# Output projection and second feed-forward of a transformer layer with token tiles as the stationary operand

## The chip, the cores and the metric

The kernel runs on one core of a Trainium2 chip. The metric is the device time of one execution in microseconds (us). A core has five engines with instruction queues of their own: PE (TensorE, matmuls, with weight loads shown as PEld), DVE (VectorE), ACT (ScalarE), POOL (GpSimd) and SP, which here starts DMAs. Matmuls write to PSUM, eight banks of 128 x 512 floats; everything else is kept in SBUF.

## The reference, cut to what matters

One layer on 256 latent tokens (and 256 context tokens, which end after the keys and values), width 2048, in float32:

```
x   = half_ffn(x, mod, 0, ...)                       # first ff, also for ctx
h   = modulate(rms_norm(x, g1), shift, scale)
q, k, v, hy = split(h @ w_in)
attn = attention(q, k, v)                            # 256 x 1024
hyo  = hyena(hy)                                     # 256 x 1024
y    = concat([rms_norm(attn, g_out[:1024]), rms_norm(hyo, g_out[1024:])])
x   = x + gate5 * (y @ w_out)                        # 2048 x 2048
h   = modulate(rms_norm(x, g2), shift6, scale7)
x   = x + 0.5 * gate8 * ((silu(h @ w_gate) * (h @ w_up)) @ w_down)   # 2048 -> 2 x 5632 -> 2048
```

The gates, shifts and scales are vectors over the 2048 features, computed from the conditioning inputs. A group's rms_norm divides each token by the root mean square over that group's 1024 features and multiplies each feature by its gain.

## The kernel before

All matrix products run in fp32r, each float split in a high part and a low rest; a product is hi*hi + hi*lo + lo*hi. Weights come from HBM in pieces of 512 KB (128 x 1024 floats, tile `raw`, four buffers, issued by SP). ACT casts the high part (`whi`, L192) and DVE, or for every second piece of the second ff's down POOL, subtracts it for the rest (`wlo`, L194); both have three buffers.

The residual `xs` is feature-major: 16 feature tiles of 128 partitions (`xd(0, d)`, L106) with the tokens along the free axis. A matmul holds a 128 x 128 piece of weights in the array and streams tokens. The first ff has latent and context tokens, 512 columns, three matmuls a piece (`mm3`, L201 to L203). From the Hyena projection on there are 256 tokens, and `mm2` (L205) streams the high and low parts of the tokens side by side past `whi` (512 columns, L209) and the high part alone past `wlo` (256 columns, L208 or L211): a pair per piece. The key/value and query projections (`proj_steps`, L644) already hold tokens in the array and stream 512 weight columns (L653 to L655).

The stages, in order: first ff; keys and values; Hyena projection (eight column tiles `ct`, L751); long convolution by DFT, with the queries in its gaps; attention, with the x0 gate of the Hyena branch filled in (`gate`, `fill`, FILL); the group norms (`group_out`, L877: squares on ACT, sums by a matmul against `ones` at L245, root and reciprocal on 128 x 256, scaling at L883, split at L181/L182); the output projection (`out_part`, L901, eight pairs of output tiles, the first three begun on the attention half alone); the norm of x (`col_rstd`), the modulation (L251 to L254) and the second ff. That one (`most`, L347) runs 44 up steps `j` of 64 pairs and after every fourth a down group of 64 pairs, whose 16 results are each multiplied by the gate and added to `xs` on DVE (L330, two per tile). Finished feature tiles are stored at the end.

Instructions are issued by Python in program order, but a scheduler of the tile framework then sets the order on each engine; engines run in that order and wait on semaphores. Tiles with tag `u` share 58 buffers of 2 KB per partition, PSUM has four `pa` and four `pb` banks.

Of the kernel before, what the change touches and what calls it, by code (L numbers as in the profile page):

```python
# [18 lines left out]
P = 128  # L19
D = 2048  # L20
# [6 lines left out]
OUT = (KT // 2, P, 2, L)  # L27
# [10 lines left out]
FILL = (1, 0, 3)  # L38
# [9 lines left out]
def hybrid_layer_kernel(ctx: ExitStack, tc: tile.TileContext, a):  # L48
# [220 lines left out]
    class Ffn:  # L269
        def __init__(self, nparts, wup, wdown, cm, hook=None):  # L270
            self.np, self.N, self.wup, self.wdown, self.cm = nparts, nparts * L, wup, wdown, cm
            self.hook = hook or (lambda: None)
            self.h = [None] * KT
            self.acts = {}
            self.gated = nparts == 1
            self.mm = mm2 if nparts == 1 else mm3
# [16 lines left out]
        def close(self, j, ps2):  # L293
            sg = tmp2((P, 2, L))
            if self.np == 2:
                S.activation(sg, ps2[0], AF.Silu)
                V.tensor_mul(sg, ps2[1], sg)
                self.acts[j] = split(sg, (P, 2, L))
                return
            for half in range(2):  # L300
                S.copy(sg[:, half, :], ps2[half][:, 1, :])
                V.tensor_add(sg[:, half, :], ps2[half][:, 0, :], sg[:, half, :])
            S.activation(sg[:, 0, :], sg[:, 0, :], AF.Silu)
            V.tensor_mul(sg[:, 1, :], sg[:, 0, :], sg[:, 1, :])
            self.acts[j] = U((P, 2, L), F32R)
            split_to(sg[:, 1, :], self.acts[j][:, 0, :], self.acts[j][:, 1, :])
# [7 lines left out]
        def down(self, g, parts=None, last=None):  # L314

            whole = parts is None
            for dq in range(KT // 2):
                self.hook()
                whi, wlo = weight(self.wdown[g, dq], (P, GRP, 2, P), G if dq % 2 and self.np == 1 else None)
                for i2 in range(2):  # L320
                    d = dq * 2 + i2
                    ps = PB((P, 2, L) if whole else (P, L))
                    for jj in range(GRP):
                        act = self.acts[g * GRP + jj]
                        if not whole:
                            act = [t[:, parts, :] for t in act]
                        self.mm(ps, (whi[:, jj, i2, :], wlo[:, jj, i2, :]), act, jj == 0, jj == GRP - 1)
                    if self.np == 1:
                        for half in range(2):
                            V.scalar_tensor_tensor(xd(0, d), ps[:, half, :], mod[0][8][:, d : d + 1], xd(0, d),  # L330
                                                   op0=ALU.mult, op1=ALU.add)
                        if last:
                            last(d)
                        continue
# [12 lines left out]
        def most(self, first):  # L347

            for j in range(first, JT):
                self.up(j)  # L350
                if j % GRP == 0 and j > 0:
                    self.down(j // GRP - 1)
# [132 lines left out]
    f1 = Ffn(2, a["w_up1"], a["w_dn1"], 0)  # L485
# [108 lines left out]
    mp = ctx.enter_context(tc.tile_pool(name="mp", bufs=1))  # L594
# [62 lines left out]
    def small(shape):  # L657
        return T(mp, shape, "small", bufs=8)

# [91 lines left out]
    for ct in range(CT):  # L751
# [5 lines left out]
        V.tensor_mul(vT[ct // 2][:, ct % 2, :], yv, y1)  # L757

# [118 lines left out]
    def group_out(src, g0, out):  # L877
        r_ = U((P, L))
        yield from rstd_steps(src, HW, r_)
        for i in range(4):  # L880
            t = T(up, (P, 2, L), "sq", bufs=2)
            for j in range(2):
                V.scalar_tensor_tensor(t[:, j, :], src[i][:, j, :], gout[:, g0 + 2 * i + j : g0 + 2 * i + j + 1], r_,  # L883
                                       op0=ALU.mult, op1=ALU.mult)
            for j in range(2):
                hl = U((P, 2, L), F32R)
                split_to(t[:, j, :], hl[:, 0, :], hl[:, 1, :])
                out.append(hl)
        yield

    y = []
    attn_out = group_out(attnT, 0, y)
    next(attn_out)
    fill(FILL[2])
    next(attn_out)
    for _ in gate:
        pass
    gate_out = group_out(hyT, CT, y)
    next(gate_out)

    def out_part(ps, dq, kqs):  # L901
        for kq in kqs:
            whi, wlo = weight(a["w_o"][dq, kq], (P, 4, 2, P))
            for i2 in range(2):
                for k4 in range(4):
                    k = kq * 4 + k4
                    mm2(ps[i2], (whi[:, k4, i2, :], wlo[:, k4, i2, :]), y[k], k == 0, k == KT - 1)

    def out_add(ps, dq):
        for i2 in range(2):  # L910
            d = dq * 2 + i2
            for half in range(2):
                V.scalar_tensor_tensor(xd(0, d), ps[i2][:, half, :], mod[0][5][:, d : d + 1], xd(0, d),
                                       op0=ALU.mult, op1=ALU.add)

    early = 3
    pso = [[f((P, 2, L)), f((P, 2, L))] for f in (PA, PA, PB)]
    for dq in range(early):
        out_part(pso[dq], dq, (0, 1))
        if dq == 0:  # L920
            next(gate_out)
    for dq in range(early):
        out_part(pso[dq], dq, (2, 3))
        out_add(pso[dq], dq)
    for dq in range(early, KT // 2):
        ps = [PA((P, 2, L)), PA((P, 2, L))]
        out_part(ps, dq, (0, 1, 2, 3))
        out_add(ps, dq)


    rs2 = U((P, L))
    col_rstd(xs[0], D, rs2)
    f2 = Ffn(1, a["w_up2"], a["w_dn2"], 6)
    f2.h = normed(0, rs2, 6)
    f2.most(0)

    def store(d):
        if d >= KT - 2:
            nc.sync.dma_start(a["out"][d // 2, :, d % 2, :], xd(0, d))
        elif d % 2:  # L940
            nc.sync.dma_start(a["out"][d // 2], xs[0][d // 2])

    f2.down(JT // GRP - 1, None, store)


# [37 lines left out]
def _prepare(i):  # L983
# [31 lines left out]
    for n in (1, 2):  # L1015
        d[f"w_up{n}"] = pair(i[f"w_ffn{n}_up"][0], JT)
        d[f"w_dn{n}"] = down(i[f"w_ffn{n}_down"][0])
# [5 lines left out]
    d["w_o"] = wide(i["w_out"][0])  # L1023
# [32 lines left out]
```

## Time and profile before

| | |
|---|---|
| median of three runs | 2728.03 us (2726.80 to 2729.72) |
| the profiled execution | 2727.58 us |
| its span | 2725.7 us |
| TensorE clock granted, mean | 0.993 |
| HBM read | 506.98 MB, 188 GB/s over the span |
| first ff until about | 1545 us |
| key/value projections to the end of attention | 1545 to 1843 us |
| group norms and output projection | 1843 to 1959 us |
| second ff | 1968 to 2722 us |

A row of the timeline gives the start and the duration of an instruction (or of several merged, x4), its engine, line and operation, what it writes and reads by name (numbers of buffers left out), and in brackets how long the engine was idle before it and who ended that. Matmuls are pipelined, so their durations overlap, and the distance of starts is what one costs. A row of the groups gives count, busy time, mean nanoseconds of one, and idle time before them. A row of the windows gives the stretch, its length, busy time and count of PE, the granted clock and the DMA share.

### The profile page before, as it was taken

What the parts mean: (1) busy time and instruction counts of PE and PEld (TensorE: products, weight loads), DVE (VectorE), ACT (ScalarE), POOL (GpSimd) and SP (SyncE); (2) the same over time, 40 slices, a digit from 0 to 9 for tenths busy, and PEclk for the clock granted to TensorE, in tenths of its full rate; (3) what the DMA queues carried; (4) which work ended last, traced back from release to release, by engine and by line L of the source; (5) the groups of instructions that cost most, each with busy time, mean ns of one, the idle gap of its engine ahead of it and who ended that gap; (6) DMA issues with size and microseconds to landing.
All of it is one profiled execution on the core that took longest, in us unless ns stands there. A gap on an engine that the chain in (4) does not pass through costs nothing.

```text
span 2725.7 us, 35248 instructions
## 1 busy us (share of the span) xinstructions
PE 2677.7 (98%) x13552; PEld 2231.1 (82%) x13552; DVE 1870.3 (69%) x3106; ACT 963.0 (35%) x1307; POOL 108.7 (4%) x51
## 2 busy tenths in 40 slices
PE   8999999999999999999999999998999999999999
PEld 5678888888888888888888878887788888888888
DVE  6589898976696666433343886988666666666666
ACT  4343222222222222222222555465454444444443
POOL 0000000000000000000000000000011111111111
PEclk9999999999999999999999999999999999999999
DMA  9776666665686666432323455333455555555555
GB/s 383 284 267 211 225 215 218 214 231 202 228 290 236 212 220 215 160 100 93 101 93 101 134 176 186 116 116 132 155 179 187 185 185 185 186 186 185 185 185 170
DMA packets 144352, 513.49 MB, mean 188 GB/s; under 512 B 17175, under 2 KB 21432, under 8 KB 139832
## 3 DMA queue, kind: packets, MB, share of 16 engines
q1 hardware_dynamic: 142456, 508.50, 54.8%
q10 hardware_dynamic: 1728, 2.74, 0.3%
q8 instruction: 107, 1.75, 0.3%
q14 instruction: 61, 0.50, 0.1%
HBM read 506.98 MB, written 4.19 MB: 188 GB/s over the span
## 4 chain that ended last, share of the span: by engine, by line
PE 94%; DVE 5%; DMA 1%; ACT 1%; issue 0%; ACTq 0%; SPq 0%; DVEq 0%
PE pa L209 17%; PE pa L203 11%; PE pa L201 11%; PE pa L202 11%; PE pa L211 8%; PE pb L201 7%; PE pb L203 7%; PE pb L202 6%; PE pb L209 6%; PE pb L211 2%; DVE u L182 1%; PE pa L654 1%; PE pa L655 1%; PE pb L157 1%; PE pa L653 1%; PE pb L208 1%
## 5 line engine op out<-in xcount | busy, mean ns | idle before, releaser
L192 ACT CAST whi<-raw 128x1024 fp32r<-128x1024 f32 x648 | 680.8, 1051 | 1310.2 <-PE pa L202 469.9
L194 DVE TENSOR_TENSOR wlo<-raw,whi 128x1024 fp32r<-128x1024 f32 x601 | 734.5, 1223 | 507.4 <-ACT whi L192 495.7
L209 PE MATMUL pa<-u,whi 128*128 128x512 f32 x2016 | 713.6, 400 | 12.7 <-DVE u L254 5.9
L201 PE MATMUL pa<-u,whi 128*128 128x512 f32 x1376 | 537.8, 392 | 0.9 <-ACT u L529 0.9
L202 PE MATMUL pa<-u,whi 128*128 128x512 f32 x1376 | 536.8, 390 | 0.7 <-DVE u L531 0.7
L203 PE MATMUL pa<-u,wlo 128*128 128x512 f32 x1376 | 535.6, 390 | 1.5 <-DVE wlo L194 1.5
L211 PE MATMUL pa<-u,wlo 128*128 128x256 f32 x1890 | 532.4, 282 | 0.8 <-DVE wlo L194 0.8
L209 PEld LDWEIGHTS pa<-u,whi 128*128 128x128 f32 x2016 | 377.2, 189 | 100.6 <-issue 6.3
L211 PEld LDWEIGHTS pa<-u,wlo 128*128 128x128 f32 x1890 | 358.9, 190 | 4.8 <-DVE wlo L194 1.7
L201 PEld LDWEIGHTS pa<-u,whi 128*128 128x128 f32 x1376 | 258.6, 188 | 58.4 <-issue 3.5
L203 PEld LDWEIGHTS pa<-u,wlo 128*128 128x128 f32 x1376 | 258.3, 188 | 57.0 <-DVE wlo L194 2.4
L202 PEld LDWEIGHTS pa<-u,whi 128*128 128x128 f32 x1376 | 259.0, 188 | 55.3 <-DVE u L531 1.6
L201 PE MATMUL pb<-u,whi 128*128 128x512 f32 (+1 forms) x800 | 298.7, 374 | 0.3 <-ACT u L176 0.3
L203 PE MATMUL pb<-u,wlo 128*128 128x512 f32 (+1 forms) x800 | 296.9, 372 | 1.0 <-DVE wlo L194 1.0
L202 PE MATMUL pb<-u,whi 128*128 128x512 f32 (+1 forms) x800 | 297.5, 372 | 0.0
L209 PE MATMUL pb<-u,whi 128*128 128x512 f32 x736 | 250.4, 399 | 2.2 <-DVE u L330 2.2
L130 DVE CUSTOM_DVE_ANT_0 adas<-adaw,crow,bada 128x1024 bf16<-128x1024 f32 x160 | 205.1, 1282 | 17.9 <-DMA adaw<-in_w_adaT_dram 15.8
L130 DVE CUSTOM_DVE_ANT_0 adas<-adaw,crow,mod 128x1024 bf16<-128x1024 f32 x160 | 205.2, 1283 | 10.4 <-DMA adaw<-in_w_adaT_dram 7.4
L194 POOL TENSOR_TENSOR wlo<-raw,whi 128x1024 fp32r<-128x1024 f32 x44 | 107.7, 2448 | 2607.7 <-ACT whi L192 2607.7
L201 PEld LDWEIGHTS pb<-u,whi 128*128 128x128 f32 x800 | 150.8, 189 | 31.5 <-issue 4.8
L203 PEld LDWEIGHTS pb<-u,wlo 128*128 128x128 f32 x800 | 150.4, 188 | 27.5 <-DVE wlo L194 1.2
L202 PEld LDWEIGHTS pb<-u,whi 128*128 128x128 f32 x800 | 150.9, 189 | 26.1
(202 smaller groups left out, 2249.6 us busy)
## 6 DMA issues: line engine op xcount, KB each, us to landing
raw<-in_w_up_dram SPq DMA_DIRECT2D x352, 512.0 KB, 3.6
adaw<-in_w_adaT_dram SPq DMA_DIRECT2D x223, 512.0 KB, 4.9
raw<-in_w_dn_dram SPq DMA_DIRECT2D x184, 512.0 KB, 3.5
wrow<-in_w_ada_dram SPq DMA_DIRECT2D x32, 1024.0 KB, 7.9
raw<-in_w_hy_dram SPq DMA_DIRECT2D x32, 512.0 KB, 3.5
raw<-in_w_o_dram SPq DMA_DIRECT2D x32, 512.0 KB, 3.5
raw<-in_w_kv_dram SPq DMA_DIRECT2D x16, 512.0 KB, 3.5
raw<-in_w_q_dram SPq DMA_DIRECT2D x16, 512.0 KB, 3.5
```

Of the source, the lines that this page charges most:

```text
L130: V.tensor_tensor_reduce(out=sc, in0=t, in1=crow[i][:, b * (D // 2) : (b + 1) * (D // 2)], scale=1.0, scalar=mcol if b else bada[:, n : n ...
L157: PE.matmul(bank[g : g + 32, 0 : 2 * P], cs[:, k, :], t[:, k8, :], start=k < 4, stop=k >= KT - 4)
L182: V.tensor_sub(lo, src, hi.bitcast(F32))
L192: S.copy(hi, raw)
L194: (eng or V).tensor_sub(lo, raw, hi.bitcast(F32))
L201: PE.matmul(ps, w[0], xx[0], start=start, stop=False)
L202: PE.matmul(ps, w[0], xx[1], start=False, stop=False)
L203: return PE.matmul(ps, w[1], xx[0], start=False, stop=stop)
L208: PE.matmul(ps[:, 0, :], w[1], x[:, 0, :], start=start, stop=False)
L209: PE.matmul(ps, w[0], x, start=start, stop=stop)
L211: PE.matmul(ps[:, 0, :], w[1], x[:, 0, :], start=False, stop=False)
L653: PE.matmul(p_, hh, whi[:, k2, :], start=k == 0, stop=False)
```

## The change

The output projection and the second ff take the form of `proj_steps`: `tok_mm` holds 128 tokens of one feature tile in the array and streams 512 weight columns, three matmuls for each of two token halves. Their results are token-major (128 tokens x 512 features), and so is the residual from there on: during the Hyena projection PE transposes it, one group of four 128 x 128 tiles per `ct`, into `xt`. The gates 5 and 8 are transposed too, written to HBM and loaded as rows broadcast over all partitions (`gate_row`).

The group norms move to the read-out: `group_in` only multiplies by the gain and splits; `group_rstd` sums the squares per token with two-column matmuls, and `out_add` multiplies the finished 128 x 512 block by the token's factor and the gate row and adds it to `xt`. The projection is eight units: four column blocks for the attention half, then four for the Hyena half. The norm of x comes from squares with a row sum (128 x 2 values per factor), and the normed x is transposed back for the array. Sixteen small matmuls (`AWAKE2`) follow the last of the projection.

The second ff runs 22 up units of 512 columns (256 of the gate half, 256 of the up half), transposes each unit's product during the next unit, and keeps all activations in SBUF; then down runs in four column blocks over all 44 activation tiles, each summed in PSUM to its end, multiplied by the gate row, added to `xt` and stored. POOL splits no weights any more.

```diff
-FILL = (1, 0, 3)
+FILL = (1, 0)
+AWAKE2 = 16
+EXTRA = 14
...
+    def turn_x(t, b):
+        ps = PB((P, 4, P))
+        for i in range(4):
+            PE.transpose(ps[:, i, :], xd(0, 4 * b + i)[:, t * P : (t + 1) * P], ident)
+        xt[t][b] = U((P, 512))
+        S.copy(xt[t][b], ps.rearrange("p a b -> p (a b)"))
...
+        turn_x(ct % 2, ct // 2)
+        if ct == 4:
+            turn_gates()
...
-    def group_out(src, g0, out):
-        r_ = U((P, L))
-        yield from rstd_steps(src, HW, r_)
...
+    def group_in(src, g0):
...
+                S.activation(hl[:, 0, :], src[i][:, j, :], AF.Copy, scale=gout[:, k : k + 1])
+                V.scalar_tensor_tensor(hl[:, 1, :], src[i][:, j, :], gout[:, k : k + 1], hl[:, 0, :].bitcast(F32),
+                                       op0=ALU.mult, op1=ALU.subtract)
+            sq = (tmp2 if i == 0 else tmp)((P, 2, L))
+            S.activation(sq, src[i], AF.Square)
...
+    def group_rstd(acc):
+        ps = PB((P, 2, 2))
+        for t in range(2):
             for j in range(2):
+                PE.matmul(ps[:, t, :], acc[:, j, t * P : (t + 1) * P], ones[:, 0:2], start=j == 0, stop=j == 1)
...
+    def tok_mm(ps, x, w, start, stop):
+
+        for t in range(2):
+            hi, lo = (x_[:, t * P : (t + 1) * P] for x_ in x)
+            PE.matmul(ps[t], hi, w[0], start=start, stop=False)
+            PE.matmul(ps[t], hi, w[1], start=False, stop=False)
+            last = PE.matmul(ps[t], lo, w[0], start=False, stop=stop)
+        return last
...
+    def out_add(ps, r_, b):
+        for t in range(2):
+            o = tmp2((P, 512))
+            V.scalar_tensor_tensor(o, ps[t], r_[:, t : t + 1], grow[b], op0=ALU.mult, op1=ALU.mult)
+            V.tensor_add(xt[t][b], xt[t][b], o)
...
+    for b in range(NB):
+        ps, last = out_unit(1, b)
+        out_add(ps, rh, b)
+        for t in range(2):
+            S.activation(tmp((P, 512)), xt[t][b], AF.Square, accum_out=sumsq[:, t, b : b + 1])
...
+    spin = PA()
+    with tc.issue_after(last.ins):
+        for _ in range(AWAKE2):
+            last = PE.matmul(spin[:, 0:P], ones, ones, start=True, stop=True)
...
+            for i in range(2):
+                d = 4 * b + 2 * i2 + i
+                sc, sh = mod[0][7][:, d : d + 1], mod[0][6][:, d : d + 1]
+                hl, m_ = U((P, 2, L), F32R), T(up, (P, L), "mt", bufs=3)
+                S.activation(hl[:, 0, :], pt[:, i, :], AF.Identity, bias=sh, scale=sc)
+                V.tensor_scalar(m_, pt[:, i, :], sc, sh, op0=ALU.mult, op1=ALU.add)
+                V.tensor_sub(hl[:, 1, :], m_, hl[:, 0, :].bitcast(F32))
...
+            if kp == 2 and prev:
+                turn_act(*prev)
+        at = U((P, 2, L))
+        for t in range(2):
+            sg = tmp2((P, L))
+            S.activation(sg, ps[t][:, 0:L], AF.Silu)
+            V.tensor_mul(at[:, t, :], ps[t][:, L : 2 * L], sg)
...
+        for t in range(2):
+            o = tmp2((P, 512))
+            V.tensor_mul(o, ps[t], grow[b])
+            V.tensor_add(xt[t][b], xt[t][b], o)
+            nc.sync.dma_start(a["out"][t, :, b * 512 : (b + 1) * 512], xt[t][b])
```

Three places of the new order. First PE within up of the second ff, before: `pa` are the PSUM tiles of one up step, `u` an input feature tile, `whi` and `wlo` the weights.

```order
L209 MATMUL pa_2967_15592<-u_2935_15512,whi_2970_15596 128x512
L211 MATMUL pa_2967_15592<-u_2935_15512,wlo_2971_15597 128x256
L209 MATMUL pa_2968_15593<-u_2935_15512,whi_2970_15596 128x512
L211 MATMUL pa_2968_15593<-u_2935_15512,wlo_2971_15597 128x256
L209 MATMUL pa_2967_15592<-u_2937_15517,whi_2970_15596 128x512
```

And now, in the second up unit, at the sixth of its sixteen k-tiles; `pb_3055` takes the transposes of the unit before (`u_3041`):

```order
L924 MATMUL pa_3045_15748<-whi_3053_15787,u_2984_15506 128x512
L925 MATMUL pa_3045_15748<-wlo_3054_15788,u_2984_15506 128x512
L926 MATMUL pa_3045_15748<-whi_3053_15787,u_2984_15506 128x512
L1011 MATMUL pb_3055_15803<-ident_1_67,u_3041_15740 128x128 x4
L924 MATMUL pa_3044_15747<-whi_3059_15814,u_2987_15516 128x512
L925 MATMUL pa_3044_15747<-wlo_3060_15815,u_2987_15516 128x512
```

Pairs of 512 and 256 columns have become triples of 512, and four transposes stand once per unit in PE's queue.

Second DVE where the output projection begins, before: `L182` are low parts of the scaled group, `L194` weight splits, `L913` the first adds to the residual.

```order
L182 TENSOR_TENSOR u_2821_14767<-sq_2820_14764,u_2821_14767 128x256
L194 TENSOR_TENSOR wlo_2837_14864<-raw_2835_14861,whi_2836_14863 128x1024
L182 TENSOR_TENSOR u_2822_14770<-sq_2820_14764,u_2822_14770 128x256
L194 TENSOR_TENSOR wlo_2840_14886<-raw_2838_14883,whi_2839_14885 128x1024
L194 TENSOR_TENSOR wlo_2843_14912<-raw_2841_14909,whi_2842_14911 128x1024
L194 TENSOR_TENSOR wlo_2846_14934<-raw_2844_14931,whi_2845_14933 128x1024
L913 SCALAR_TENSOR_TENSOR u_32_117<-pa_2797_14675,mod0_5_19_102,u_32_117 128x256 x2
```

Now, with `L901` and `L908` of the Hyena group's `group_in`, `L941` and `L942` the read-out of the projection's first unit, and `wlo_2842` the first split of its second unit:

```order
L901 SCALAR_TENSOR_TENSOR u_2833_14821<-u_2419_13089,gout_1761_9352,u_2833_14821 128x256
L901 SCALAR_TENSOR_TENSOR u_2834_14824<-u_2419_13089,gout_1761_9352,u_2834_14824 128x256
L908 TENSOR_TENSOR sg_2826_14801<-sg_2826_14801,sq_2835_14827 128x512
L941 SCALAR_TENSOR_TENSOR sg_2836_14830<-pa_2810_14721,small_2807_14712,u_2802_14699 128x512
L941 SCALAR_TENSOR_TENSOR sg_2837_14833<-pa_2811_14722,small_2807_14712,u_2802_14699 128x512
L942 TENSOR_TENSOR u_2273_12294<-u_2273_12294,sg_2836_14830 128x512
L942 TENSOR_TENSOR u_2293_12406<-u_2293_12406,sg_2837_14833 128x512
L200 TENSOR_TENSOR wlo_2842_14841<-raw_2840_14838,whi_2841_14840 128x1024
```

The splits of the next unit stood ahead of the first adds; now its first split stands behind the group's work and the whole read-out.

Third PE at the joint from the projection to the second ff, before: `pb_2924` is the sum of squares of x.

```order
L211 MATMUL pa_2910_15382<-u_2821_14767,wlo_2922_15452 128x256
L208 MATMUL pa_2910_15382<-u_2822_14770,wlo_2922_15452 128x256
L209 MATMUL pa_2910_15382<-u_2822_14770,whi_2921_15451 128x512
L245 MATMUL pb_2924_15476<-sg_2925_15477,ones_2_72 128x256 x2
L245 MATMUL pb_2924_15476<-sq_2932_15497,ones_2_72 128x256 x2
L209 MATMUL pa_2967_15592<-u_2935_15512,whi_2970_15596 128x512
```

Now, with the spin at `L969` and `u_2967`, `u_2968` the normed x of the two token halves:

```order
L926 MATMUL pa_2945_15343<-whi_2956_15400,u_2834_14824 128x512
L969 MATMUL pa_2962_15430<-ones_2_72 128x128 x16
L991 MATMUL pb_2969_15462<-ident_1_67,u_2967_15458 128x128
L991 MATMUL pb_2974_15477<-ident_1_67,u_2967_15458 128x128
L991 MATMUL pb_2969_15462<-ident_1_67,u_2968_15460 128x128
L991 MATMUL pb_2969_15462<-ident_1_67,u_2967_15458 128x128
L991 MATMUL pb_2969_15462<-ident_1_67,u_2968_15460 128x128
L991 MATMUL pb_2974_15477<-ident_1_67,u_2968_15460 128x128
L991 MATMUL pb_2974_15477<-ident_1_67,u_2967_15458 128x128
L991 MATMUL pb_2974_15477<-ident_1_67,u_2968_15460 128x128
L924 MATMUL pa_3015_15594<-whi_3018_15598,u_2970_15467 128x512
```

The two sums over all features are gone from PE; sixteen small matmuls and eight transposes of the normed x stand between the projection and the first up matmul.

More of the change, by code (lines that the diff above doesn't have):

```diff
@@ L294, in close @@
             sg = tmp2((P, 2, L))
[L295 to L306, printed above, removed]
+            S.activation(sg, ps2[0], AF.Silu)
+            V.tensor_mul(sg, ps2[1], sg)
+            self.acts[j] = split(sg, (P, 2, L))
         def up(self, j):
@@ L318, in down @@
                 self.hook()
-                whi, wlo = weight(self.wdown[g, dq], (P, GRP, 2, P), G if dq % 2 and self.np == 1 else None)
+                whi, wlo = weight(self.wdown[g, dq], (P, GRP, 2, P))
                 for i2 in range(2):
@@ L658, in small, with turn_gates, gate_row @@
         return T(mp, shape, "small", bufs=8)
+    xt = [[None] * NB for _ in range(2)]
+    def turn_x(t, b):
[4 more added lines that the diff above has]
+        S.copy(xt[t][b], ps.rearrange("p a b -> p (a b)"))
+    gate_rows = T(dram, (2, KT, P), "gate_rows")
+    def turn_gates():
+        ps, rows = PB((KT, 2, P)), tmp((KT, 2, P))
+        for n, c in enumerate((5, 8)):
+            PE.transpose(ps[:, n, :], mod[0][c], ident)
+        S.copy(rows, ps)
+        nc.scalar.dma_start(gate_rows.rearrange("n k p -> k n p"), rows)
+    def gate_row(n):
+        out = []
+        for b in range(NB):
+            out.append(U((P, 512)))
+            nc.sync.dma_start(out[b], gate_rows[n : n + 1, 4 * b : 4 * b + 4, :].rearrange("n k p -> n (k p)").partition_broadcast(P))
+        return out
     def head_norm(ps, nh):
@@ new lines, in tok_mm, with out_unit @@
+    def tok_mm(ps, x, w, start, stop):
[5 more added lines that the diff above has]
+        return last
+    def out_unit(g, b):
+        ps = [PA(), PA()]
+        for kp in range(4):
+            whi, wlo = weight(a["w_o"][b, 4 * g + kp], (P, 2, 512))
+            for k2 in range(2):
+                k = 2 * kp + k2
+                last = tok_mm(ps, [y[8 * g + k][:, s, :] for s in range(2)], (whi[:, k2, :], wlo[:, k2, :]), k == 0, k == 7)
+        return ps, last
@@ L896, in hybrid_layer_kernel @@
+    def out_add(ps, r_, b):
[3 more added lines that the diff above has]
+            V.tensor_add(xt[t][b], xt[t][b], o)
+    acc = group_in(attnT, 0)
     for _ in gate:
         pass
[L898 to L907, printed above, removed]
@@ L925, in hybrid_layer_kernel @@
[L925 to L943, printed above, removed]
+    grow = gate_row(0)
@@ L1022, in _prepare @@
     d["w_x0"] = wide(c_(wi[:, 1536:2560]))
-    d["w_o"] = wide(i["w_out"][0])
+    d["w_o"] = np.stack([cols(c_(i["w_out"][0][:, b * 512 : (b + 1) * 512])) for b in range(NB)])
     def eo(v):
```

140 lines of the change are left out of this document (91 added, 49 removed).

## The prediction

> **What bounds the kernel now.** I read the page first (busy time, then the chain that ended last), then windows for whole stages, then the timeline for the distance from one matmul's start to the next.
>
> ```profile
> span 2725.7 us, 35248 instructions
> PE 2677.7 (98%) x13552; PEld 2231.1 (82%) x13552; DVE 1870.3 (69%) x3106; ACT 963.0 (35%) x1307; POOL 108.7 (4%) x51
> PE 94%; DVE 5%; DMA 1%; ACT 1%; issue 0%; ACTq 0%; SPq 0%; DVEq 0%
> ```
>
> TensorE (PE) is the engine of the chain; only what it streams, and the places where it stands still, count. Busy time overlaps from one matmul to the next, so I go by starts. First nine matmuls in a row of the key/value projection, which already has tokens standing and 512 weight columns moving; then nine pairs of the second ff's old form (weights standing, 512 and 256 token columns moving).
>
> ```profile
> 1602.96 0.39 PE L653 MATMUL pa<-whi,u 128*128 128x512 f32 x1
> ...
> 1605.00 0.39 PE L653 MATMUL pa<-whi,u 128*128 128x512 f32 x1
> ```
>
> ```profile
> 2199.66 0.40 PE L209 MATMUL pa<-u,whi 128*128 128x512 f32 x1
> 2199.89 0.28 PE L211 MATMUL pa<-u,wlo 128*128 128x256 f32 x1
> ...
> 2202.84 0.40 PE L209 MATMUL pa<-u,whi 128*128 128x512 f32 x1
> ```
>
> (1605.00 - 1602.96) / 9 = 0.2267 us per 512-column matmul; (2202.84 - 2199.66) / 9 = 0.3533 us per pair of 512 + 256.
>
> **The stream itself.** Call a block 128 rows by 512 columns of weights, for all 256 tokens. Before, it is four pairs, 4 x 0.3533 = 1.413 us; now six matmuls of 512, 6 x 0.2267 = 1.360 us. The columns streamed are equal (3072); what goes is two starts, 0.053 us a block. Blocks: 16 x 4 = 64 in the projection, 16 x 22 = 352 in up, 44 x 4 = 176 in down; 592 x 0.053 = 31.4 us is the gain from this alone.
>
> The Trainium skill, "TensorE: Matmul & The Clock Gate", section "Back-to-back issue gap", speaks against that: it gives N/2.4 + 2.5 ns, by which four pairs are 1.300 us and six matmuls 1.295, so 592 x 0.005 = 3 us in all. The trace disagrees with its fixed 2.5 ns, with 226.7 ns at 512 columns, so I keep the measured rows.
>
> **Turned inputs.** The new form needs transposes on PE. Four of them among 512-column matmuls:
>
> ```profile
> 1758.74 0.40 PE L655 MATMUL pa<-whi,u 128*128 128x512 f32 x1
> 1758.97 0.60 PE L870 MATMUL pb<-ident,u 128*128 128x128 f32 x4
> 1759.32 0.48 PE L653 MATMUL pa<-whi,u 128*128 128x512 f32 x1
> ...
> 1760.81 0.39 PE L654 MATMUL pa<-wlo,u 128*128 128x512 f32 x1
> ```
>
> Seven 512-column matmuls start from 1758.74 until before 1760.81: 2.07 us where seven alone take 1.59, so a group of four costs 0.48 us, the slower restart included. Bounds: 0.36 (four starts of 0.09) and 0.60 (the four's own duration). The residual is turned in 8 groups in the Hyena projection, where PE has no slack, with two more for the gates: 8 x 0.48 + 0.25 = **+4.1 us**. ACT's eight copies and the gate rows' DMAs lie beside it: the loads of 256 KB stand on SP among weights of 512 KB, four buffers ahead of their use.
>
> **Attention's end and the projection.** The stretch from 1838.39 to the first matmul of the final norm at 1959.12 is 120.7 us:
>
> ```profile
> L209 PE MATMUL pa<-u,whi 128*128 128x512 f32 x258 | 92.1, 404 | 6.8 <-DVE sg L731 5.7 <-ACT whi L192 1.0
> L209 PE MATMUL pb<-u,whi 128*128 128x512 f32 x32 | 11.2, 395 | 0.0
> L245 PE MATMUL pb<-sg,ones 128*128 128x256 f32 x9 | 2.5, 387 | 2.1 <-DVE sg L241 2.1
> 1959.12 1.03 PE L245 MATMUL pb<-sg,ones 128*128 128x256 f32 x4
> L201 PE MATMUL pb<-u,u 128*128 128x512 f32 x4 | 1.7, 420 | 0.5 <-DVE u L177 0.5
> L194 DVE TENSOR_TENSOR wlo<-raw,whi 128x1024 fp32r<-128x1024 f32 x601 | 734.5, 1223 | 507.4 <-ACT whi L192 495.7
> L883 DVE SCALAR_TENSOR_TENSOR sq<-u,gout,u 128x256 f32<-128x256 f32 x16 | 7.3, 481 | 0.0
> L297 DVE TENSOR_TENSOR sg<-pa,sg 128x512 f32<-128x512 f32 x43 | 29.6, 690 | 69.8 <-PE pa L203 69.8
> ```
>
> 288 pairs (32 of the x0 gate, 256 of the projection; the count of 290 takes in two at the edges) are 101.8, twelve 512s of attention 2.7; 16.2 us are norms on PE (sixteen L245, about 3.8) and waiting or half-clock running (12.4). Now the norms need no wide rows: only their 8 two-column sums on PE, taken at 0.11 each, a little over a transpose. PE has 11.3 + 2.7 + 64 x 1.360 = 87.0, + 0.9. Waits that remain, by walking ACT and DVE in their new order: 1.5 before attention's last matmuls (the same conversions as before); 0.95 for the gate's last weight splits, behind group_in's scaled copies; 1.1 for the Hyena group's sum of squares, on which the second row sum waits in PE's queue with unit 1's matmuls behind it; 3.7 since unit 1's first split (1.22) stands on DVE behind group_in's 0.48s and the first four out_add operations (0.69 each). With some slower restarts 7.5; bounds 2.5 (only the first and some restarts) and 12.4 (as before). 109.4 in place of 120.7: **-11.3 us**.
>
> **The joint to the second ff.**
>
> ```profile
> 1958.88 0.40 PE L209 MATMUL pa<-u,whi 128*128 128x512 f32 x1
> 1967.80 0.77 PE L209 MATMUL pa<-u,whi 128*128 128x512 f32 x1 [5.93 <-DVE u L254]
> L234 ACT ACTIVATE sq<-u 128x512 f32<-128x512 f32 x22 | 13.8, 629 | 3.5 <-DVE sg L241 1.1 <-DVE u L819 1.1 <-DVE u L913 1.0
> L842 DVE RECIPROCAL small<-small 128x1 f32<-128x1 f32 x16 | 2.5, 159 | 0.7 <-ACT u L841 0.4
> L253 ACT ACTIVATE u<-mt,mod 128x256 fp32r<-128x256 f32 x48 | 21.4, 499 | 12.7 <-DVE mt L251 12.6
> ```
>
> Before, 8.92 us from the last projection matmul's start to up's first. Now, from that matmul's end (0.39 after its start): four 512-wide DVE operations, the first about 0.65 early since token half 0 is complete three matmuls sooner, 2.1; a square and its sum, 0.9, beside which DVE does one weight split (1.22), so 3.3; the reduce, five operations of 0.16 and the root with hand-overs, 1.4; the scaled copy 0.63; transposes at half clock 1.0; the high part 0.5: 6.9. 7.3 against 8.92: **-1.6 us** (bounds -3.5 and +1.5: one hand-over more or less at each of eight steps, and another split ahead). The 16 spin matmuls lie in it and cost nothing.
>
> Does the clock halve there?
>
> ```profile
> 1586.17 0.50 PE L654 MATMUL pa<-wlo,u 128*128 128x512 f32 x1 [2.27 <-DVE wlo L194]
> 1586.51 0.40 PE L655 MATMUL pa<-whi,u 128*128 128x512 f32 x1
> ...
> 1593.64 0.80 PE L654 MATMUL pa<-wlo,u 128*128 128x512 f32 x1 [4.42 <-DVE wlo L194]
> 1594.23 0.63 PE L655 MATMUL pa<-whi,u 128*128 128x512 f32 x1
> ...
> 1597.65 0.63 PE L655 MATMUL pa<-whi,u 128*128 128x512 f32 x1
> 1598.40 0.39 PE L654 MATMUL pa<-wlo,u 128*128 128x512 f32 x1
> ```
>
> Idle 2.27 us left the pace alone; 4.42 was followed by 4.4 us at 0.43 per matmul. The spin covers some 1.7 us (16 of 0.11), leaving about 3.6 idle, nearer to the second row: I take some 5 us of half pace, 2.5 us lost; bounds 0 and 4. The Trainium skill, "TensorE: Matmul & The Clock Gate", section "What's actually happening", puts the limit at an idle window of about 3.4 us that runs free; by it this joint could fall either way, and warm would make the sum 2.5 us less.
>
> **The second ff.** Before, from 1967.80 to the last matmul:
>
> ```profile
> 2721.44 0.39 PE L209 MATMUL pb<-u,whi 128*128 128x512 f32 x1
> L330 DVE SCALAR_TENSOR_TENSOR u<-pb,mod,u 128x256 f32<-128x256 f32 x352 | 157.2, 479 | 8.2 <-PE pb L209 3.3
> 2029.76:2097.98 68.22, 68.02 (x386) 1.00 0.56 186
> L192 ACT CAST whi<-raw 128x1024 fp32r<-128x1024 f32 x648 | 680.8, 1051 | 1310.2 <-PE pa L202 469.9
> L303 ACT ACTIVATE sg<-sg 128x256 f32<-128x256 f32 x44 | 18.3, 417 | 0.0
> L194 POOL TENSOR_TENSOR wlo<-raw,whi 128x1024 fp32r<-128x1024 f32 x44 | 107.7, 2448 | 2607.7 <-ACT whi L192 2607.7
> ```
>
> 2721.44 + 0.23 - 1967.80 = 753.9 us, of which 2112 pairs are 746.2 and the rest waits. Now 528 x 1.360 = 718.1; 22 groups of turned activations, 10.6; eight groups that turn the normed input, 3.9; half clock 2.5: 735.1, **-18.8 us**. What covers the rest: the 352 adds of 0.48 leave DVE, POOL's 44 splits come to it (44 x 1.22 = 54 us); a unit of up gives DVE 8 x 1.22 + 0.69 + 2 x 0.42 = 11.3 of 22.2 us. If DVE were full, each split would cost PE up to 1.22. The turned activations' transposes stand after the sixth k-tile, 8.2 us into the next unit, while Silu, product and hand-overs take some 3 to 5; behind them in PE's queue wait that unit's other matmuls. The first unit's inputs cost DVE about 0.9 + 0.1 + 0.6 (half a split) = 1.6 us per k-tile against PE's 1.36; three splits already done and the slow clock cover it. Weights load as before, 512 KB per 2.72 us on engines busy 0.56.
>
> **The end.**
>
> ```profile
> 2721.87 1.00 DVE L330 SCALAR_TENSOR_TENSOR u<-pb,mod,u 128x256 f32<-128x256 f32 x2 [0.40 <-PE pb L209]
> out_dram<-u SPq DMA_DIRECT2D x7, 256.0 KB, 2.0
> out_dram<-u SPq DMA_DIRECT2D x2, 128.0 KB, 1.7
> ```
>
> Two adds of 0.5 now become two products and two adds of 0.69, one of which starts before the last matmul ends: 2.05 for 1.0; the last store is 256 KB, 0.3 more: **+1.3 us**.
>
> Sum: +4.1 - 11.3 - 1.6 - 18.8 + 1.3 = -26.3. The profiled execution took 2727.58 us, so 2701.3; the median of the runs, 2728.03, is 0.45 above it: **2702**.
>
> **Rivals.** 0.2%, 5.5 us, is about what a measurement of this kernel can tell from no change.
> (a) The new form does not keep its pace when it runs for 700 us: six matmuls take what four pairs take. Then 31.4 is gone: 2733, no change by that bound. For it: the restart after transposes is slower than 0.2267. Against: the rows at 1602.96, the same form and operands. By the Trainium skill's formula of "Back-to-back issue gap" it would be 2702 + 28 = 2730, the same side. Chance 0.04.
> (b) Slower: the turned activations come late. PE takes instructions in order; if Silu and product sat behind casts on ACT and splits on DVE until more than 8.2 us into the next unit, each microsecond beyond costs 22. From 9.6 us on it is slower than before (22 x 1.43 = 31.5); at 9.8, 2737. Against: ACT has 8 x 1.05 + 2 x 0.42 + 0.6 = 9.8 us of work in 22.2. Chance 0.03.
> (c) The waits at the projection do not shrink, or DVE starves up's first unit: 5 us dearer, 2707, still faster. Chance 0.18.
> That the change does not do what it says is out: the order on PE shows the six-matmul form throughout.
> My forecast has 0.72; 0.03 is left for larger gains. The range 2693 to 2713 takes in 2.5 to 12.4 of waits at the projection, 0.36 to 0.60 for 38 groups of transposes (-4.6, +4.6) and the clock, not all at one end; it holds (c). Faster 0.93, same 0.04, slower 0.03.
>
> **What would show it.** L924 to L926 spaced 0.2267 us in up and down; 22 gaps of about 0.48 at L1011; the first up matmul 7.3 us after the projection's last; half pace for some 5 us there; fewer than 8 us of waits between attention and projection. Wrong: a spacing near 0.235, or PE waiting at L1011 for DVE.

## The result and the profile after

The changed kernel takes 2701.7 us, median of 4 runs (2699.76 to 2702.6); the kernel before, on the same chip, 2727.6 (2726.8 to 2729.72). The ratio is 0.9904, 95% interval 0.9888 to 0.992. The forecast was 2702. The page's head and the chain that ended last, of the changed kernel:

```profile
span 2698.0 us, 32497 instructions
PE 2659.2 (99%) x12546; PEld 2183.8 (81%) x12546; DVE 1725.1 (64%) x2689; ACT 941.0 (35%) x1215; POOL 1.0 (0%) x7
PE 95%; DVE 3%; DMA 1%; issue 0%; ACT 0%; SPq 0%; ACTq 0%; DVEq 0%
```

PE issues 1006 instructions fewer and still sets the end; DVE's share of the chain fell from 5% to 3%. To see where the time went I laid the same marks into both traces. Timeline of PE, kernel before: the second step of the Hyena projection, the first DFT transposes, and the last full matmul of the gate ahead of attention's last products (the later marks are in the prediction).

```profile
1626.98 0.28 PE L211 MATMUL pa<-u,wlo 128*128 128x256 f32 x1
...
1705.86 1.03 PE L777 MATMUL pb<-ident,u 128*128 128x128 f32 x8
...
1838.39 0.39 PE L209 MATMUL pa<-u,whi 128*128 128x512 f32 x1
```

The same view of the changed kernel, with the last matmul of the projection, the filler and the first transposes behind it, the first of up and the very last:

```profile
1626.56 0.28 PE L217 MATMUL pa<-u,wlo 128*128 128x256 f32 x1
...
1708.17 1.04 PE L791 MATMUL pb<-ident,u 128*128 128x128 f32 x8
...
1843.77 0.39 PE L215 MATMUL pa<-u,whi 128*128 128x512 f32 x1
...
1951.09 0.40 PE L926 MATMUL pa<-whi,u 128*128 128x512 f32 x1
1951.33 3.73 PE L969 MATMUL pa<-ones 128*128 128x128 f32 x32
1956.64 1.11 PE L991 MATMUL pb<-ident,u 128*128 128x128 f32 x8 [1.58 <-DVE u L985]
1958.08 0.50 PE L924 MATMUL pa<-whi,u 128*128 128x512 f32 x1 [0.33 <-ACT u L996]
...
2692.39 0.39 PE L926 MATMUL pa<-whi,u 128*128 128x512 f32 x1
```

Differences between neighbouring marks give each stretch, in us:

| stretch | before | after | difference | forecast |
|---|---|---|---|---|
| start to the Hyena projection's second step | 1626.98 | 1626.56 | -0.4 | +0.5 |
| rest of the Hyena projection | 78.88 | 81.61 | +2.7 | +3.6 |
| DFT, queries, attention | 132.53 | 135.60 | +3.1 | 0 |
| attention's end and projection | 120.49 | 107.32 | -13.2 | -11.3 |
| joint, last projection matmul to first of up | 8.92 | 6.99 | -1.9 | -1.6 |
| second ff, first to last matmul | 753.64 | 734.31 | -19.3 | -18.8 |
| last matmul to the end of the span | 4.26 | 5.61 | +1.4 | +1.3 |

They add up to -27.7, the difference of the spans; the medians differ by 25.9. Two gate pairs (0.7 us) have moved from the third stretch into the fourth, so its loss is nearer 3.8 and the gain behind it nearer 13.9. The first row is no gain: the work up to there differs by one group of transposes only, and the profiles of the changed kernel and of the seven variants below, alike up to the first group, reach it up to 4.0 us apart (1625.89 to 1629.91). So profiles are compared by stretch and runs by their medians.

### The profile page after: what moved, and what is told of

The parts are those of the page before. It is cut to its first block, busy times and chain, and to the rows that moved or that the text cites. A ratio compares the mean times of both kernels' runs of the same rounds, so it can differ in the third digit from the quotient of the medians.

```text
span 2698.0 us, 32497 instructions
## 1 busy us (share of the span) xinstructions
PE 2659.2 (99%) x12546; PEld 2183.8 (81%) x12546; DVE 1725.1 (64%) x2689; ACT 941.0 (35%) x1215; POOL 1.0 (0%) x7
## 4 chain that ended last, share of the span: by engine, by line
PE 95%; DVE 3%; DMA 1%; issue 0%; ACT 0%; SPq 0%; ACTq 0%; DVEq 0%
PE pa L209 12%; PE pa L208 12%; PE pa L207 11%; PE pa L926 10%; PE pa L925 10%; PE pa L924 10%; PE pb L207 7%; PE pb L209 7%; PE pb L208 7%; PE pa L215 3%; PE pa L217 2%; PE pa L638 1%; PE pb L163 1%; PE pa L639 1%; PE pa L637 1%; DVE wlo L200 1%
## 5 line engine op out<-in xcount | busy, mean ns | idle before, releaser
L200 DVE TENSOR_TENSOR wlo<-raw,whi 128x1024 fp32r<-128x1024 f32 x645 | 788.6, 1224 | 681.1 <-ACT whi L198 675.3
L207 PE MATMUL pa<-u,whi 128*128 128x512 f32 x1376 | 537.4, 391 | 2.9 <-ACT u L512 2.9
L208 PE MATMUL pa<-u,whi 128*128 128x512 f32 x1376 | 536.6, 390 | 0.7 <-DVE u L514 0.7
L925 PE MATMUL pa<-wlo,u 128*128 128x512 f32 x1072 | 418.4, 390 | 1.9 <-DVE wlo L200 1.9
L924 PE MATMUL pa<-whi,u 128*128 128x512 f32 x1072 | 419.6, 392 | 0.3 <-ACT u L996 0.3
L926 PE MATMUL pa<-whi,u 128*128 128x512 f32 x1072 | 418.4, 391 | 0.0
L207 PEld LDWEIGHTS pa<-u,whi 128*128 128x128 f32 x1376 | 258.2, 188 | 60.4 <-ACT u L512 4.2
L209 PEld LDWEIGHTS pa<-u,wlo 128*128 128x128 f32 x1376 | 258.1, 188 | 57.4 <-DVE wlo L200 2.9
L208 PEld LDWEIGHTS pa<-u,whi 128*128 128x128 f32 x1376 | 258.7, 188 | 55.3 <-DVE u L514 1.6
L925 PEld LDWEIGHTS pa<-wlo,u 128*128 128x128 f32 x1072 | 201.8, 188 | 43.4 <-DVE wlo L200 2.0
L926 PEld LDWEIGHTS pa<-whi,u 128*128 128x128 f32 x1072 | 201.5, 188 | 43.0 <-DVE u L998 1.0
L924 PEld LDWEIGHTS pa<-whi,u 128*128 128x128 f32 x1072 | 201.6, 188 | 41.7 <-ACT u L996 0.6
```

Source lines behind the costliest of these rows:

```text
L200: (eng or V).tensor_sub(lo, raw, hi.bitcast(F32))
L207: PE.matmul(ps, w[0], xx[0], start=start, stop=False)
L208: PE.matmul(ps, w[0], xx[1], start=False, stop=False)
L209: return PE.matmul(ps, w[1], xx[0], start=False, stop=stop)
L924: PE.matmul(ps[t], hi, w[0], start=start, stop=False)
L925: PE.matmul(ps[t], hi, w[1], start=False, stop=False)
```

## The new form keeps its pace

PE's timeline within one unit of up, the changed kernel:

```profile
2058.28 0.39 PE L926 MATMUL pa<-whi,u 128*128 128x512 f32 x1
2058.51 0.60 PE L1011 MATMUL pb<-ident,u 128*128 128x128 f32 x4
...
2061.94 0.39 PE L925 MATMUL pa<-wlo,u 128*128 128x512 f32 x1
...
2062.39 0.39 PE L924 MATMUL pa<-whi,u 128*128 128x512 f32 x1
...
2066.93 0.39 PE L926 MATMUL pa<-whi,u 128*128 128x512 f32 x1
```

Twenty starts from 2062.39 to 2066.93 are 0.227 us each: the row of the key/value projection carried over to the second ff. From 2058.28 to 2061.94 stand fourteen matmuls and one group of transposes: 3.66 - 14 x 0.2267 = 0.487 us for the group, its slower restart included. A unit of up takes 22.247 us from one group to the next, 16 x 1.360 + 0.487. DVE's product, on which the group waits, has long ended:

```profile
2050.96 0.42 DVE L1028 TENSOR_TENSOR u<-pa,sg 128x256 f32<-128x256 f32 x1 [0.25 <-ACT sg L1027]
```

2058.51 - 2051.38 = 7.1 us of slack. Rival (b) never came near; the product is ready about 1 us into the next unit, not 3 to 5.

To see what the gain per block consists of, three kernels cut the third matmul of each three back into two of 256 columns, which makes eight starts a block again.

```
 e3    PE.matmul(ps[t], hi, w[0], ...)
      +PE.matmul(ps[t][:, 0:L], lo, w[0][:, 0:L], ...)
       PE.matmul(ps[t], hi, w[1], ...)
      -last = PE.matmul(ps[t], lo, w[0], ...)
      +last = PE.matmul(ps[t][:, L : 2 * L], lo, w[0][:, L : 2 * L], ...)
 e6   the same, both halves behind the second 512
 e7   as e3, but both halves take and write columns 0 to 255
```

> In projection and second ff the third matmul of each three (low part of the activations against 512 weight columns) is cut into two of 256 columns, standing behind the first and the second 512: eight starts a block of 128 rows by 512 columns as in the kernel before, same products. Theory 1 (only the number of starts costs): 4 x 0.2267 + 4 x 0.1195 = 1.385 us a block against 1.360, 592 blocks, +14.7 us, 2716 us. Theory 2 (the price of the alternating pair of the kernel before, 0.3533 us, holds whatever stands): 1.413 a block, +31.4 us, 2733 us. Theory 3 (the old form was slow for its operands, not for its lengths): no change, 2702 us.

> As the alternating halves, but the two matmuls of 256 columns stand behind both of 512 (512, 512, 256, 256), the same products. Alternating cost 18.5 us, 0.031 a block, where starts alone explain 14.7. Theory (what is left is the price of following a 512 by a 256): 14.7 us dearer than the changed kernel or a little less, 2716 us. Rival (alternation costs nothing): as alternating, 2720 us.

> As the alternating halves, but both matmuls of 256 columns take and accumulate into the left half of the columns, as the kernel before did with its high half; the low part of the activations is thus counted twice in the left half of the columns and left out of the right half. The kernel before paid 1.413 us a block, the alternating halves 1.391, the changed kernel 1.360. Theory (accumulating into the half that the matmul ahead and the one behind also write is what the old form paid besides its starts): 0.022 a block more than alternating, 13 us, 2733 us. Rival (the place written does not matter): 2720 us; the rest of the old form's price then has to do with something else.

Measured: together 2716.85 us (2716.25 to 2718.45; ratio to before 0.9958, interval 0.9945 to 0.997), alternating 2720.17 (2719.24 to 2721.48; 0.9972, 0.9961 to 0.9983), left 2720.24 (2718.02 to 2723.68; 0.9971, 0.9959 to 0.9982). Together is 15.2 dearer than the changed kernel, where the two extra starts were priced at 14.7; alternating costs another 3.3; the half of the columns written makes no difference. By the traces, from the first projection matmul to the last matmul, they are 17.1, 20.1 and 20.0 us longer than the changed kernel. PE's timeline in up, halves together: fourteen rounds of four from the first row to the second.

```profile
2190.20 0.40 PE L924 MATMUL pa<-whi,u 128*128 128x512 f32 x1
...
2199.95 0.40 PE L924 MATMUL pa<-whi,u 128*128 128x512 f32 x1
```

And halves alternating, twelve pairs ahead of the group of transposes at 2200.48, then six pairs behind it:

```profile
2185.16 0.28 PE L925 MATMUL pa<-whi,u 128*128 128x256 f32 x1
...
2189.40 0.28 PE L925 MATMUL pa<-whi,u 128*128 128x256 f32 x1
...
2201.27 0.39 PE L926 MATMUL pa<-wlo,u 128*128 128x512 f32 x1
...
2203.35 0.39 PE L926 MATMUL pa<-wlo,u 128*128 128x512 f32 x1
```

Together: 9.75 / 14 = 0.696 a round, 1.393 a block. Alternating: 4.24 / 12 = 0.3533 a pair ahead of the group, 1.413 a block, and 2.08 / 6 = 0.3467 behind it, 1.387. The pace changes so at every group of up, where the stretches from one group to the next take 23.05 and 22.64 us in turn; a group itself costs 23.05 - 16 x 1.413 = 0.44 us, against 0.487 among 512s. So of the 0.053 us that a block gained, 0.025 are two starts by the rows and some 0.008 more the company of the two lengths. The alternating form has two paces, one the old 1.413, the other nearly the two starts alone (1.385), and 1.400 on average. That it costs 18.5 us in all and not 31.4 has several reasons: half of up runs at the quicker pace (352 x 0.013 = 4.6 us), its 22 groups are 1.0 us cheaper, and a block of down takes about 1.397, only 0.026 more than in the changed kernel (1.371).

The changed kernel itself shows this switch where it still runs pairs, in the Hyena projection: twenty pairs take 7.06 us from 1628.45 and, behind the next group of transposes, 6.94 us from 1640.16. Where the groups stand two and two (early turning, below), the pairs behind each two stay at 0.3467. So four transposes mostly flip the pace of the pairs behind them, with a few exceptions in the traces; why is not settled.

The Trainium skill, "TensorE: Matmul & The Clock Gate", section "Back-to-back issue gap", gives N/2.4 + 2.5 ns for an isolated matmul; by it the change was worth 3 us here. These runs disagree: 592 blocks with two starts more are 15.2 us by the medians, some 13 ns a start.

## The loss in the DFT stage

No step of the prediction had this: the trace of before shows no wait there, and the stretch was taken over at no change. PE's timeline of the changed kernel has three:

```profile
1754.24 0.39 PE L207 MATMUL pb<-u,u 128*128 128x256 f32 x1 [0.63 <-ACT u L182]
...
1756.00 0.39 PE L209 MATMUL pb<-u,u 128*128 128x256 f32 x1 [0.54 <-DVE u L183]
...
1761.26 0.47 PE L637 MATMUL pa<-whi,u 128*128 128x512 f32 x1 [1.65 <-DVE u L680]
```

2.8 us, and the restarts. They name DFT splits and the query norm. What runs late on ACT and DVE are the splits of the four DFT matrices, which are constants. ACT's timeline, before and then after:

```profile
1698.45 0.62 ACT L176 CAST u<-dftc 128x512 fp32r<-128x512 f32 x1
```

```profile
1710.19 0.57 ACT L652 COPY u<-pb 128x512 f32<-128x512 f32 x1
1710.66 0.62 ACT L182 CAST u<-dftc 128x512 fp32r<-128x512 f32 x1
```

ACT takes its instructions in order, and the copy of the last turned group now stands ahead of these casts. That copy needs the transposes behind the last matmul of the Hyena projection, so the casts that used slack on ACT and DVE inside the projection fall behind it, 12 us later, among the DFT's own conversions. The test is to turn the residual earlier:

```
-    turn_x(ct % 2, ct // 2)
+    if ct < NB:
+        turn_x(0, ct)
+        turn_x(1, ct)
```

> The residual's eight groups of transposes and copies are issued two per step in the first four steps of the Hyena projection, in place of one per step in all eight. Theory (ACT's order): in the changed kernel ACT's copy of the last turned group, which waits for PE's transposes at 1707.74 us, stands ahead of the casts of the four DFT matrices, so these begin at 1710.66 us where the kernel before began them at 1698.45; PE then waits 0.91, 0.82 and 1.92 us among the DFT and query matmuls (1753 to 1761 us), about 3.3 us with the slower restarts. With the copies early the casts run about 1700 us, those waits go, and the time is 2698.5 us (3.2 less than 2701.7). Rival (the transposes themselves or the eight buffers they hold): the waits stay, 2701.7 us within 0.7.

Measured: 2697.8 us (2696.17 to 2700.47; ratio to before 0.9891, interval 0.9877 to 0.9904), 3.9 less than the changed kernel. ACT's timeline has the cast back in the projection, and the three waits are gone:

```profile
1700.63 0.62 ACT L182 CAST u<-dftc 128x512 fp32r<-128x512 f32 x1
```

From the first DFT transposes to the first projection matmul it is 145.59 us against 149.12, 3.5 of the 3.9. The eight groups and the eight buffers they hold are as many as before, so the rival falls: the order was the cause.

## The wait at the projection

In the changed kernel PE waits once between attention and the last projection matmul. PE's timeline there, and its granted clock by windows (columns: window, length, busy time of PE, PEld, DVE, ACT and POOL, clock, DMA share, GB/s):

```profile
1871.10 0.95 PE L915 MATMUL pb<-ones,sg 128*128 128x2 f32 x8
1873.98 0.80 PE L925 MATMUL pa<-wlo,u 128*128 128x512 f32 x1 [1.94 <-DVE wlo L200]
...
1877.13 0.41 PE L924 MATMUL pa<-whi,u 128*128 128x512 f32 x1
```

```profile
1874.00:1877.00 3.00, 3.00 (x7) 2.44 (x8) 2.27 (x3) 0.00 (x0) 0.00 (x0) 0.50 0.73 202
```

For 2.9 us PE has only the row sums, which stream two columns each (0.95 us), and then a wait of 1.94; behind it the clock is halved for 3.15 us, in which seven matmuls take 1.56 more than at full pace. DVE's timeline shows what the split is queued behind:

```profile
1868.62 0.88 DVE L901 SCALAR_TENSOR_TENSOR u<-u,gout,u 128x256 fp32r<-128x256 f32 x2
1869.41 0.69 DVE L908 TENSOR_TENSOR sg<-sg,sq 128x512 f32<-128x512 f32 x1
1870.16 1.43 DVE L941 SCALAR_TENSOR_TENSOR sg<-pa,small,u 128x512 f32<-128x512 f32 x2
1871.51 1.28 DVE L942 TENSOR_TENSOR u<-u,sg 128x512 f32<-128x512 f32 x2
1872.71 3.49 DVE L200 TENSOR_TENSOR wlo<-raw,whi 128x1024 fp32r<-128x1024 f32 x3
```

The split of unit 1's first weight piece stands behind group_in's last operations and the four of out_add, as the prediction had it (3.7 us there). The first edit put each unit's residual update behind the second of the next unit's four pieces; pieces() is out_unit() that calls hooks[kp] behind piece kp:

```
 for b in range(NB):
-    ps, _ = out_unit(0, b)
-    if b == 0:
-        acch = group_in(hyT, CT)
-    out_add(ps, ra, b)
+    hooks = {}
+    if b == 0:
+        hooks[1] = [lambda: acch.append(group_in(hyT, CT))]
+    if prev:
+        hooks[1] = [lambda p=prev: out_add(p, ra, b - 1)]
+    prev, _ = pieces(0, b, hooks)
```

> In the projection each pair of residual updates is issued after the second weight piece of the next unit, in place of right behind its own unit; likewise the Hyena group's preparation and its row sums. Theory (DVE's order): PE stood still for 3.9 us at 1870 us since the first weight split of unit 1 was queued on DVE behind four updates (2.7 us), and ran eight matmuls at 0.43 us behind it (1.6 us dearer). With the updates behind the splits about 1.2 us of wait is left (the group's preparation still stands ahead) and no half pace: 4.3 us less, 2697.4 us. Rival (DVE is simply full there): the wait moves to a later unit, at most 1 us is gained, 2700.7 to 2701.7 us.

Measured: 2700.83 us (2698.67 to 2701.81; ratio 0.99, interval 0.9886 to 0.9913), 0.9 less than the changed kernel where 4.3 was expected: the rival's time. (The 3.9 us of standing still in that expectation are 2.9 by the rows above.) PE's timeline, then ACT's:

```profile
1867.37 0.61 PE L924 MATMUL pa<-whi,u 128*128 128x512 f32 x2
1869.88 0.74 PE L924 MATMUL pa<-whi,u 128*128 128x512 f32 x2 [1.89 <-ACT whi L198]
```

```profile
1868.28 0.61 ACT L904 ACTIVATE sq<-u 128x512 f32<-128x512 f32 x1
1868.80 1.03 ACT L198 CAST whi<-raw 128x1024 fp32r<-128x1024 f32 x1
```

The wait moved from the fifth weight piece to the third, and from DVE to ACT: the Hyena group's preparation (eight scaled copies and four squares on ACT, eight differences and three sums on DVE) now stood ahead of that piece. The half clock is gone, and first to last projection matmul fell from 93.8 to 92.4 us. So the updates were only the last of what was queued, and the theory fell. Either DVE is full there, or the preparation is bunched; cutting it into four steps, one to a unit, tells these apart. It stands on both edits above; group_in, as more_y, now yields after each of its four steps.

```
-    hooks = {}
-    if b == 0:
-        hooks[1] = [lambda: acch.append(group_in(hyT, CT))]
+    hooks = {2: [lambda: acch.append(next(more_y))]}
```

> The early turning of the residual and the late updates together, and the Hyena group's preparation (scaled copies, squares, sums) cut into four steps, one behind the third weight piece of each of the first four units. In the late updates alone the wait only moved: PE still stood from 1867.83 to 1871.27 us, first for ACT's cast and then for DVE's split of the third piece, both queued behind that preparation. Theory (the preparation, 5.6 us on DVE and some 6 on ACT, bunched ahead of the splits, is what PE waits for): spread out, wait and half pace both go, first to last projection matmul falls from 93.8 to about 89.5 us, and the time is 2693.5 us (2697.8 of the early turning less 4.3). Rival (DVE is full over these units whatever the order): only the 1.4 us that the late updates gained, 2696.4 us.

Measured: 2693.79 us (2691.87 to 2695.78; ratio to before 0.987, interval 0.9855 to 0.9885), as the theory had it. PE's waits from the DFT to the last projection matmul, changed kernel and then this one:

```profile
PE pa L925 <- DVE wlo L200: 1.9, 1, 1.9
PE pa L637 <- DVE u L680: 1.6, 1, 1.6
PE pa L217 <- DVE wlo L200: 0.6, 1, 0.6
PE pb L207 <- ACT u L182: 0.6, 1, 0.6
PE pb L209 <- DVE u L183: 0.5, 1, 0.5
PE pb L864 <- DVE u L857: 0.3, 1, 0.3
```

```profile
PE pa L217 <- DVE wlo L200: 0.6, 1, 0.6
PE pb L866 <- DVE u L859: 0.3, 1, 0.3
```

Four of the six waits are gone; the two that stay lie ahead of the projection and are the same in both. First to last projection matmul is 90.2 us. DVE was not full; the work came in one lump. The spreading was not run without the late updates, so the 4.0 us gained over early turning belong to the two together. This kernel takes 7.9 us less than the changed one and 34 less than before.

## The joint and the clock

The prediction let the 16 filler matmuls cover 1.7 us, and so expected 3.6 idle and half pace behind it. The row of L969 above shows 32 passes in 3.73 us: each of these plain f32 matmuls runs as two. The trace of before showed it already: the sums of squares at the joint are two times two matmuls in its order of instructions and two times four in its timeline (1959.12, x4). PE then stood for 1.58 us, by the row of L991, and the first up matmuls start 0.23 apart, at full pace. Without the filler (AWAKE2 = 0):

> The 16 filler matmuls between the projection and the second ff are left out (they write nothing that is used). The changed kernel's trace shows them as 32 passes that fill 3.6 of the 5.5 us, with 1.9 us idle behind them and full pace from the first up matmul. Theory (an idle time near 5 us halves the clock, as 4.42 did and 2.27 did not before the key/value projection): about ten matmuls at 0.43 us, 2.2 us dearer, 2704 us, and the trace shows the half pace. Rival (the clock is set otherwise, or the first unit's own waits on DVE hide it): 2701.7 us within 0.7.

Measured: 2704.24 us (2701.05 to 2705.49; ratio to before 0.9912, interval 0.9898 to 0.9925), 2.5 more than with it. PE's timeline and the windows, where the clock is the last figure but two:

```profile
1960.10 1.99 PE L991 MATMUL pb<-ident,u 128*128 128x128 f32 x8 [5.16 <-DVE u L985]
1961.89 0.79 PE L924 MATMUL pa<-whi,u 128*128 128x512 f32 x1
...
1966.08 0.42 PE L924 MATMUL pa<-whi,u 128*128 128x512 f32 x1
```

```profile
1962.00:1966.00 4.00, 4.00 (x10) 2.87 (x10) 3.75 (x9) 2.20 (x4) 0.00 (x0) 0.50 0.00 0
```

Behind an idle time of 5.2 us the clock is halved until 1966.08. The price in this profile is 0.36 us at the transposes and 1.4 in up's first unit. The medians' 2.5 and the spread of these runs do not contradict that.

The length of the idle time alone does not decide it. In the trace of halves left the filler stands as in the changed kernel, and up begins at half pace all the same (PE's timeline, then a window):

```profile
1961.84 1.11 PE L992 MATMUL pb<-ident,u 128*128 128x128 f32 x8 [1.53 <-DVE u L986]
```

```profile
1964.00:1967.00 3.00, 2.82 (x9) 2.34 (x9) 2.82 (x8) 2.03 (x4) 0.00 (x0) 0.50 0.00 0
```

Its first unit of up takes 27.0 us, against 25.8 in the two other kernels with halves. So the filler kept the pace in six of the seven traces that have it. In every trace the granted clock changes only on a raster of 3.41 us (here it is halved from 1963.74 to 1967.15), so where a pause falls on this raster probably counts too; no run tests that. The Trainium skill, "TensorE: Matmul & The Clock Gate", section "What's actually happening", puts the limit at an idle window of about 3.4 us that runs free. The raster agrees with it, and so do full pace behind 1.6 us of idling and half pace behind 5.2; half pace behind 1.5 does not, if the window has to be idle from end to end.

## Right and wrong, step by step

- **The stream** was right in its rows: 0.2267 a matmul, 1.360 a block, no rival (a). That only starts go was too simple: they are about half to two thirds of the 0.053 a block.
- **Turned inputs, +4.1**: mis-sized. Seven groups and the gates took 2.7, so (2.7 - 0.25) / 7 = 0.35 a group, and +3.1 in all. That this is the lower bound named (four bare starts) is chance: a group itself cost about 0.43 there (1625.89 to 1626.56, less 0.24 for the one 512 in it), but in every second stretch the 32 pairs behind it ran at 0.3467 in place of 0.3533, which gave 0.2 us back. The price of 0.48 came from a group among 512s, and held in up, where its neighbours are 512s.
- **"ACT's eight copies ... lie beside it"** failed. The copies' time was hidden; their place in ACT's order was not. It cost 3.1 to 3.8 us in a stage that the sum had left out, and early turning gave 3.9 back.
- **Attention's end and projection, -11.3**: -13.2, or -13.9 with the two gate pairs. The wait behind group_in and out_add was there, 1.9 us instead of 3.7, with 1.6 of half pace that had been lumped into restarts. The 1.5 ahead of attention's last matmuls did not come: in the changed kernel they start 0.12 us behind the gate's. The two-column sums took 0.95 us for each group's four, about twice what was put down, since they too run as two passes.
- **The joint, -1.6**: -1.9, by its chain of steps.
- **Half clock, 2.5 lost**: failed, as the filler was counted at half its length; 0 was lost in the changed kernel's trace. Its price was about right, as leaving the filler out showed (1.8 by the trace, 2.5 by the medians).
- **Second ff, -18.8**: -19.3, by errors on both sides. The half clock (2.5) did not come, and two of the eight groups that turn the normed input were counted twice, here and as 1.0 us in the joint: the row of L991 x8 stands ahead of up's first matmul, so six groups were left. So 22.3 were to be expected. Of the 3.0 that are missing, about 0.9 went in up's first unit (25.5 us, where 96 matmuls and six groups are 24.7) and 1.9 in down, where each of the four column blocks begins with 84 matmuls at 0.232 us and goes on at 0.2267. These 84 are exactly those that hold `act` tiles, the first 14 activation tiles, which have buffers of their own (EXTRA); the others hold `u`. No run tests whether that is the cause. And what the prediction took for waits in the old form (753.9 less 746.2) was to some 3 us half clock: the kernel before ran up at half pace until 1973.74, so these 3 us of the gain are the clock's and not the stream's.
- **The end, +1.3**: +1.4.

That the median met the forecast within a microsecond is luck: the missed loss (+3.1), what down (1.9) and up's first unit (0.9) took stood against sizes that came out cheaper: turning 1.0, projection 1.9, half clock 2.5, and the 1.0 counted twice.

## What to carry to other kernels

When work is added to an in-order engine, price its place besides its time: list what stands behind it there, and ask what that used to do while the engine waited. A wait "behind" the last operation queued is rarely cured by moving that one; look at how long the whole queue ahead has been running, and spread it. Among matmuls of equal columns, the longest form saves a start each, here some 13 ns, and a price taken from a row holds only among the neighbours which that row has. A filler is sized by what the trace shows of it, and not by its count of instructions.

## What the runs showed that was not expected

- A matmul of plain f32 operands (L969, L915) stands in the trace as two passes; 128 columns took 0.111 us each.
- Four transposes cost 0.43 to 0.44 us among pairs of 512 and 256, and 0.487 among 512s. Among pairs they mostly flip the pace behind them, between 0.3467 and 0.3533 a pair.
- All six traces that have PE's wait behind the row sums (1.7 to 1.94 us behind 0.95 us of two-column sums; 1873.98 in the changed kernel) show half pace behind it; a wait of 1.89 us behind 512s (late updates, 1869.88) was not followed by it. So such sums may not keep the clock up. But this last wait, from 1867.98 to 1869.88, falls into two slots of the clock's raster (the edge is at 1869.32), which would explain it as well. No run tells these apart.
